# Queries and keys of the attention loaded through SyncE's hardware queue as plain 32-bit numbers

## The chip, the core and the metric

The kernel runs on one core of a Trainium2 chip. A core has TensorE (PE, matrix products), VectorE (DVE), ScalarE (ACT), GpSimd (POOL) and SyncE (SP), and 16 DMA engines that move data between its on-chip memory (SBUF, 128 partitions) and DRAM. SP issues transfers through the hardware queue, GpSimd through the software queue. The metric is the time of one execution on the chip, in microseconds (us); lower is better.

## What is computed

One layer of a decoder trunk over 1040 tokens (16 learned ones and 1024 of the sequence), width 1024. Four mixers work on columns of one projection: windowed attention (A), differential attention (B), a recurrent mixer (C, RWKV-7) and a convolution module (D). Then come an output projection, a router and 16 experts.

```python
u = h @ w_in
ya = swa_attention(qa, ka, va, sinks, rel_a)     # 4 query heads on 2 key heads, 64 wide, window 128
yb = diff_attention(qd, kd, vd, lam, ...)        # 4 heads, two softmax maps each, 32 wide
yc = rwkv7_mix(uc, ...)                          # state carried from chunk to chunk
yd = conv_module(ud, ...)
h = LN(alpha * h + concat(ya, yb, yc, yd) @ w_out)
h = LN(alpha * h + moe(h))
```

The change concerns the inputs of A and B: their queries and keys.

## The kernel before

The kernel has three stages. The first (to about 257 us) normalises the input and computes the recurrent mixer's and the convolution's projections. The second holds the attention's projections, the recurrence in 17 chunks of 64 tokens, the attention over 8 blocks of 128 queries, and the output projection with the router. The third, from about 1000 us, runs the experts. Their weights stream through SP's queue.

In the second stage a planner (`Steps.run`) sets the order of the work. Each piece of work is a step with an engine, a guessed cost, what it depends on, and the buffers that it takes (`RINGS`, `SZ`). The planner always takes the step that can start first by its own guesses, and writes its instructions at that place. So the order on every engine is fixed when the program is built. An engine works strictly in that order and stands still where an instruction's data isn't there, whatever could run behind it.

The path of queries and keys. `project` and `qk_evac` compute them in parts: ScalarE writes the rounded part `qhi` (type float32r), VectorE the remainder `qlo`, and SP stores both to the DRAM array `dqk` [7, 2, 128, 1040] (L869, L870), as float32. Each row is 1040 numbers, 4160 bytes. After the last projection `load_qk` (L1280) reads them back, one step for each of six head groups `s`: 0 and 1 are the windowed attention's two key heads, 2 to 5 the four differential heads. Each group fills four buffers `qk0` to `qk3` of 128 partitions and 1040 numbers. Groups 0 and 1 do it in four transfers of 128 rows, groups 2 to 5 in eight of 64 rows. The source is read with an outermost count of 2, for instance the two remainders behind each other (`[WS, 2]`) or the same rows twice (`[0, 2]`). The buffers have the type float32r and the source float32; a transfer that changes the type goes through GpSimd's software queue. `SZ["qk0"]` to `SZ["qk3"]` are 2, so two groups are on the chip at a time.

The order of use (`ORDER`): groups 0 and 2 together, block by block; then groups 1 and 3; then 4 and 5. The scores are computed at L1340 and L1341 (windowed) and at L1444 and L1424 (differential). Between them stand pieces of the recurrence: `prep` (L928 to L1013) and `chain` (L1045 to L1105), whose inputs SP loads at L903 and L904. `values` (L1254) loads the attention's values.

DMAs of one queue share eight semaphores in turn, so the ninth transfer is issued once the first has landed.

Of the kernel before, what the change touches and what calls it, by code (L numbers as in the profile page):

```python
# [9 lines left out]
F32 = mybir.dt.float32  # L10
# [15 lines left out]
NT = S + M  # L26
# [166 lines left out]
def build(tc, A, out, dbg=None, upto=99):  # L193
# [3 lines left out]
    V, G, ACT, T, SY = nc.vector, nc.gpsimd, nc.scalar, nc.tensor, nc.sync  # L197
# [492 lines left out]
    a = add("DVE", .1, lambda: V.memset(relx, NEG), (), TB)  # L690
# [14 lines left out]
    a = add("DVE", .7, tb_neg, [tl_], TB)  # L705
# [26 lines left out]
    a = add("Pool", 1.6, empty, [tl_], TB, use=[scy])  # L732
# [60 lines left out]
    st_ = Steps(RINGS)  # L793
# [16 lines left out]
    def at_(name, shape, dt=F32):  # L810
        return ap_.tile([P] + shape, dt, name=name, bufs=RINGS.get(name) or SZ[name])
# [300 lines left out]
    class Norms:  # L1112
# [5 lines left out]
        def add(self, y, deps):  # L1118
            add, pr = st_.add, self.pr
            w, s1_, s2_, w.s3 = O(), Slot("tp"), Slot("tp"), Slot("sq")  # L1120
            w.y = y

            def a1():
                w.a = bank2("tp")
                T.matmul(w.a, bdm, y, start=True, stop=True)

            def a2():
                V.tensor_tensor(y, y, w.a, op=ALU.subtract)

            def a3():  # L1130
                w.sq = rt("sq", [512])
                ACT.activation(w.sq, y, AF.Square)

            def a4():
                w.a = bank2("tp")
                T.matmul(w.a, bdm, w.sq, start=True, stop=True)

            def a5():
                ACT.activation(w.sq, w.a, AF.Ln, bias=self.eps)
            a = add("PE", .9, a1, deps, pr, take=[s1_])  # L1140
            a = add("DVE", dve(512), a2, [a], pr, use=[s1_])
            a = add("ACT", act(512), a3, [a], pr, take=[w.s3])
            a = add("PE", .9, a4, [a], pr, take=[s2_], use=[w.s3])
            self.logs.append(add("ACT", act(512), a5, [a], pr, use=[s2_, w.s3]))
            self.w.append(w)
            return w
# [131 lines left out]
    qkb, qkl, qks = {}, {}, {}  # L1278

    def load_qk(s, deps):  # L1280
        WS = P * NT

        def ld(dst, i, w, r, n, outer):
            a = dqk[i, w, r:r + n]
            G.dma_start(dst, bass.AP(tensor=a.tensor, offset=a.offset, ap=outer + [[NT, n], [1, NT]]))  # L1285

        def go():
            t = qkb[s] = [at_(f"qk{z}", [NT], F32R) for z in range(4)]
            if s < 2:
                r = 64 * s  # L1290
                for w in range(2):
                    ld(t[w], 2, w, r, 64, [[0, 2]])
                    ld(t[2 + w], w, 0, r, 64, [[WS, 2]])
            else:
                hp_, hh_ = divmod(s - 2, 2)
                for c in range(2):
                    r = 64 * hh_ + 32 * c
                    for z in range(2):
                        ld(t[c][64 * z:64 * z + 64], 3 + hp_, 0, r, 32, [[WS, 2]])
                        ld(t[2 + c][64 * z:64 * z + 64], 5 + hp_, z, r, 32, [[0, 2]])  # L1300
        qks[s] = Slot("qk")
        qkl[s] = st_.add("Pool", 4 if s < 2 else 8, go, deps, 1, take=[qks[s]])
    for z in range(4):
        SZ[f"qk{z}"] = 2

# [283 lines left out]
    for ct in range(2):  # L1589
# [3 lines left out]
        for q, w in enumerate(cw_):  # L1593
            conv_silu(ct, q, w, last)
    sw = [st_.add("SY", 0, switch, sp_, 0)]
    load_qk(0, sw)
    tabs = [st_.add("SY", 6, tables, after, 30)]
    tabs = [st_.add("DVE", 1.6, far_bias, tabs, 5)]
    vals = sum([values(i, 0.6 + .1 * i, sw) for i in range(3)], [])
    for s in (2, 1, 3, 4, 5):  # L1600
        load_qk(s, sw)
# [44 lines left out]
    def high(i):  # L1646
        ACT.activation(slot_h[i % HLS][0], raw[i], AF.Copy)  # L1647

    def low(i, eng):
        h, l = slot_h[i % HLS]  # L1650
        eng.tensor_tensor(l, raw[i], h.bitcast(F32), op=ALU.subtract)  # L1651
        free_r.append(raw.pop(i))
# [363 lines left out]
    for i, eng in enumerate(PREL):  # L2016
        a = add("ACT", act(D), lambda i=i: high(i), (wdone if i >= NEW else []) + [raws[i]] + (sgd[-1:] if i >= HEARLY else []), SB + 20 + i)
        a = add(eng, dve(D) if eng == "DVE" else pol(D), lambda i=i, eng=eng: low(i, V if eng == "DVE" else G), [a] + ((ixd if i >= DEARLY else lnd)[-1:] if eng == "DVE" else []), SB + 20 + i)
# [187 lines left out]
    st_ = Steps(dict(st=2))  # L2206
# [45 lines left out]
    for half in range(2):  # L2252
# [3 lines left out]
        a = add("ACT", .35, lambda h=h, half=half: ACT.activation(B.act[:, h], B.a[half][:, 0:256], AF.Silu), [last], -20)  # L2256
        sl_.append(a)
        a = add("DVE", .35, lambda h=h, half=half: V.tensor_tensor(B.act[:, h], B.act[:, h], B.a[half][:, 256:512], op=ALU.mult), [a], -20)
# [6 lines left out]
        a = add("PE", .22, t1, [a], -20)  # L2265
        a = add("ACT", .3, lambda v=v, h=h: ACT.activation(B.at[:, 0, h], v.tb[:, :256], AF.Copy), [a], -20)
# [17 lines left out]
    a = add("DVE", .2, lambda: V.bn_aggr(mv[:, NB], B.st), [zs[-1]], -5, use=[zst])  # L2284
    c = add("ACT", .3, lambda: root(NB, NB + 1), [a] + sl_, -5)
    a = add("DVE", dve(D), lambda: V.scalar_tensor_tensor(B.y, B.y, mv[:, NB, 0:1], g2r, op0=ALU.subtract, op1=ALU.mult), [a], -5)
# [94 lines left out]
```

## Time and profile before

| | |
|---|---|
| median of 3 runs | 1639.62 us (1634.83 to 1651.75) |
| the profiled execution's own time | 1646.74 us |
| its span, first to last instruction | 1645.0 us |
| TensorE busy (8079 matmuls) | 1321.9 us, 80% |
| VectorE, ScalarE, GpSimd busy | 945.1, 636.3, 519.2 us |
| mean granted clock of TensorE | 0.858 of full speed |
| DMA, hardware queue | 176.25 MB, 34.2% of 16 engines |
| DMA, software queue | 41.73 MB, 14.1% of 16 engines |
| issues at L1285 on POOL | 40, 27.7 us busy, 715 ns each |

The profile is one execution. "Busy" is the time in which an engine works; issuing a DMA counts on POOL here and doesn't on SP. Other views break it down by time: the waits (who waited for whom), the timeline of an engine, and windows, which give for each stretch the busy time of every engine, the granted TensorE clock (1.00 is 2.4 GHz, 0.50 is 1.2 GHz), the mean share in which the 16 DMA engines were busy, and the GB/s that they moved.

### The profile page before, as it was taken

How to read it: one execution, taken by the hardware profiler on the slowest of the kernel's cores; microseconds unless marked ns; L12 is line 12 of the kernel's file. 1: busy time of each engine (PE TensorE's matmuls, PEld its weight loads, DVE VectorE, ACT ScalarE, POOL GpSimd, SP SyncE). 2: the span in 40 equal slices, each digit the busy share in tenths (PEclk: the TensorE clock that was granted, in tenths of full speed). 3: DMA queues.
4: the chain of work that ended last, by engine and by line, in shares of the span. 5: the costliest groups of instructions: out<-in, count | busy, mean ns of one | idle time of the engine just before them, and what ended most of it. 6: DMA issues, size and time to landing. Idle time of an engine off the chain costs nothing. (4 is left out here: it accounts for less than half of the span.)

```text
span 1645.0 us, 22192 instructions
## 1 busy us (share of the span) xinstructions
PE 1321.9 (80%) x8079; PEld 1071.5 (65%) x8079; DVE 945.1 (57%) x1628; ACT 636.3 (39%) x1108; POOL 519.2 (32%) x382
## 2 busy tenths in 40 slices
PE   6908999999859949968967885779799789978980
PEld 4807899887738738756836764557577567756860
DVE  8307658883214433646856768574744774465466
ACT  6204412323113333425663313444544554454351
POOL 3303214322110121233325233442544354344323
PEclk9958999999955767977969977779899899989995
DMA  7431246221480070090023336586877797586652
GB/s 179 88 50 65 82 119 195 82 79 54 94 123 1 17 100 23 1 105 20 2 103 117 126 77 220 158 267 197 281 230 218 227 316 229 151 262 208 203 168 115
DMA packets 186403, 220.14 MB, mean 134 GB/s; under 512 B 56903, under 2 KB 155335, under 8 KB 185976
## 3 DMA queue, kind: packets, MB, share of 16 engines
q1 hardware_dynamic: 152328, 176.25, 34.2%
q0 software_dynamic: 33904, 41.73, 14.1%
q8 instruction: 93, 1.52, 0.4%
q14 instruction: 78, 0.64, 0.1%
HBM read 172.41 MB, written 45.44 MB: 132 GB/s over the span
## 5 line engine op out<-in xcount | busy, mean ns | idle before, releaser
L452 PE MATMUL acc<-hh,wh 128*128 128x256 f32 (+2 forms) x288 | 97.8, 340 | 0.0
L452 PE MATMUL acc<-hh,wl 128*128 128x256 f32 (+2 forms) x288 | 93.7, 326 | 0.0
L1651 DVE TENSOR_TENSOR wl<-MX,wh 128x1024 fp32r<-128x1024 f32 x46 | 85.4, 1892 | 13.6 <-ACT wh L1647 13.1
L452 PE MATMUL acc<-hl,wh 128*128 128x256 f32 (+2 forms) x288 | 87.7, 323 | 0.0
L2095 PE MATMUL rw<-wh,at 128*128 128x512 f32 x224 | 81.0, 411 | 6.2 <-DVE at L2071 5.8
L1169 DVE SCALAR_TENSOR_TENSOR CY<-MX,cvw,CY 128x1024 f32<-128x1024 f32 x60 | 82.5, 1399 | 0.2
L1647 ACT ACTIVATE wh<-MX 128x1024 fp32r<-128x1024 f32 x66 | 66.3, 1048 | 10.9 <-PEq L2142 10.9
L1651 DVE TENSOR_TENSOR wol<-MX,woh 128x1024 fp32r<-128x1024 f32 x33 | 60.3, 1863 | 12.6 <-ACT woh L1647 11.0
L1462 ACT ACTIVATE E<-sc,nm 128x144 f32<-128x144 f32 (+7 forms) x64 | 48.0, 750 | 50.3 <-DVE nm L1456 45.4
L1486 POOL TENSOR_TENSOR E<-E,rho 128x272 f32<-128x272 f32 (+3 forms) x16 | 20.5, 1281 | 147.9 <-DVE rho L1480 107.1
L2099 POOL DMA_INDIRECT acc__131<-y,ixs x21 | 34.4, 1637 | 103.4 <-issue 64.7
L835 POOL TENSOR_TENSOR wl<-raw,wh 128x1024 fp32r<-128x1024 f32 x10 | 26.3, 2628 | 115.2 <-ACT wh L832 106.4
L2071 DVE TENSOR_TENSOR at<-tp,at 128x256 fp32r<-128x256 f32 x46 | 19.4, 422 | 73.7 <-ACT at L2070 73.7
L452 PEld LDWEIGHTS acc<-hh,wh 128*128 128x128 f32 x288 | 55.8, 194 | 5.8 <-issue 5.5
L1800 PE MATMUL oacc<-wol,mh 128*128 128x512 f32 x128 | 54.2, 423 | 5.8 <-POOL wol L1747 4.0
L1800 PE MATMUL oacc<-woh,mh 128*128 128x512 f32 x128 | 56.2, 439 | 1.7 <-ACT woh L1744 1.7
L1285 POOL DMA_DIRECT2D qk<-dqk x40 | 27.7, 715 | 93.6 <-DMA qk<-dqk 53.1
L452 PEld LDWEIGHTS acc<-hh,wl 128*128 128x128 f32 x288 | 55.6, 193 | 1.7 <-issue 1.0
L1647 ACT ACTIVATE woh<-MX 128x1024 fp32r<-128x1024 f32 x51 | 51.7, 1049 | 12.3 <-PEq L2142 8.5
L2095 PEld LDWEIGHTS rw<-wh,at 128*128 128x128 f32 x224 | 42.2, 191 | 18.3 <-DVE at L2071 8.4
L452 PEld LDWEIGHTS acc<-hl,wh 128*128 128x128 f32 x288 | 53.8, 190 | 0.0
L1800 PE MATMUL oacc<-woh,ml 128*128 128x512 f32 x128 | 53.4, 417 | 0.0
(474 smaller groups left out, 3923.7 us busy)
## 6 DMA issues: line engine op xcount, KB each, us to landing
MX<-in_exp_w_dram SPq DMA_DIRECT2D x192, 256.0 KB
MX<-in_exp_w_dram SPq DMA_DIRECT2D x48, 512.0 KB
CY<-in_exp_w_dram SPq DMA_DIRECT2D x64, 256.0 KB
raw<-in_w_in_dram SPq DMA_DIRECT2D x20, 512.0 KB
qk<-dqk POOLq DMA_DIRECT2D x32, 260.0 KB, 15.4
CY<-in_exp_w_dram SPq DMA_DIRECT2D x16, 512.0 KB
dab<-ab SPq DMA_DIRECT2D x2, 2176.0 KB
qk<-dqk POOLq DMA_DIRECT2D x8, 520.0 KB, 27.5
```

What stands on the lines that cost most here:

```text
L452: T.matmul(v.acc[:, :wid], wt[:, k], x[:, k, c0:c0 + wid], start=(z + y == 0 and wt is w.h), stop=(z + y == len(ks) - 1))
L835: G.tensor_tensor(w.l, w.raw, w.h.bitcast(F32), op=ALU.subtract)
L1169: V.scalar_tensor_tensor(y, hc[:, M + j:M + j + S], cvw[:, ct, j:j + 1], y, op0=ALU.mult, op1=ALU.add)
L1285: G.dma_start(dst, bass.AP(tensor=a.tensor, offset=a.offset, ap=outer + [[NT, n], [1, NT]]))
L1462: ACT.activation(w.E[:, c, off:W], w.sc[c][:, :W - off], AF.Exp, bias=w.nm[:, c:c + 1], scale=-1.0, accum_out=w.s[:, c:c + 1])
L1486: G.tensor_tensor(w.E[:, 1, :W], w.E[:, 1, :W], w.rho.to_broadcast([P, W]), op=ALU.mult)
L1647: ACT.activation(slot_h[i % HLS][0], raw[i], AF.Copy)
L1651: eng.tensor_tensor(l, raw[i], h.bitcast(F32), op=ALU.subtract)
L1800: T.matmul(v.o, x_[:, k], y_[k][:, 512 * n:512 * n + 512], start=(i == 0 and j == 0), stop=(i == KT - 1 and j == 2))
L2071: V.tensor_tensor(dst[:, 1, s], tb[:, :m * P], dst[:, 0, s].bitcast(F32), op=ALU.subtract)
L2095: T.matmul(o[n], at[:, x, k * P:(k + 1) * P], w[k][y][:, n * 512:n * 512 + 512], start=(k == 0 and (x, y) == (0, 0)), stop=(k == 3 and x = ...
L2099: G.indirect_dma_start(out=acc_, out_offset=bass.IndirectOffsetOnAxis(ap=ix[:, 0:1], axis=0), in_=y, in_offset=None, compute_op=ALU.add)
```

## The change

The 40 loads of `load_qk` are issued by SP instead of GpSimd. The destination is passed as float32 (`bitcast`), so that no type is changed in the transfer. The planner sees the step on SP, with other guessed costs.

```diff
         def ld(dst, i, w, r, n, outer):
             a = dqk[i, w, r:r + n]
-            G.dma_start(dst, bass.AP(tensor=a.tensor, offset=a.offset, ap=outer + [[NT, n], [1, NT]]))
+            SY.dma_start(dst.bitcast(F32), bass.AP(tensor=a.tensor, offset=a.offset, ap=outer + [[NT, n], [1, NT]]))
...
-        qkl[s] = st_.add("Pool", 4 if s < 2 else 8, go, deps, 1, take=[qks[s]])
+        qkl[s] = st_.add("SY", 3 if s < 2 else 5, go, deps, 1, take=[qks[s]])
```

On SP, the loads of groups 0 and 2 now stand behind the three loads of the values (the number behind `qk_` is the buffer's; 128x1x1040 is the shape written):

```order
 L1254 DMA E<-dvv 128x1040 x3
+L1285 DMA qk_3715<-dqk 128x1x1040
+L1285 DMA qk_3717<-dqk 128x1x1040
+L1285 DMA qk_3716<-dqk 128x1x1040
+L1285 DMA qk_3718<-dqk 128x1x1040
+L1285 DMA qk_3761<-dqk 64x1x1040
+L1285 DMA qk_3763<-dqk 64x1x1040
```

Six more of group 2 follow, and behind them the recurrence's next loads (L903, L904), which stood right behind L1254 before. On POOL the same loads are gone from between the recurrence's products (L1053):

```order
 L1053 TENSOR_SCALAR sp_3356<-s_3316,pend 128x64 x2
-L1285 DMA qk_3592<-dqk 128x1x1040
-L1285 DMA qk_3594<-dqk 128x1x1040
-L1285 DMA qk_3593<-dqk 128x1x1040
-L1285 DMA qk_3595<-dqk 128x1x1040
-L1053 TENSOR_SCALAR sp_3647<-s_3618,pend 128x64 x2
-L1285 DMA qk_3661<-dqk 64x1x1040
```

Since the guessed costs differ, the planner also shifts other work by a few places on every engine. On PE, where the second pair of groups is used first (group 1 at L1340, group 3 at L1444), before:

```order
L928 MATMUL prep<-abv 128x128 x4
L1506 MATMUL tp<-c__63,E 128x128 x7
L1506 MATMUL tp<-c__63,E 16x128
L982 MATMUL prep<-Tt,gs 64x64 x8
L1367 MATMUL tp<-c__63,Es 128x128 x4
L982 MATMUL prep<-X,um 64x64 x8
L1526 MATMUL tp<-vs,at 128x128 x7
L1527 MATMUL tp<-vs,at 128x128
L1068 MATMUL chain<-r,X 64x64 x4
L1375 MATMUL tp<-c__63,Es 16x128 x2
L1444 MATMUL sc<-qk_4662,qk_4660 128x144
```

These rows stand right behind the first L1340 and L1341 of group 1. In the changed kernel the same place reads:

```order
L1341 MATMUL sc<-qk_4533,qk_4535 128x144
L982 MATMUL prep<-Tt,gs 64x64 x8
L1506 MATMUL tp<-c__63,E 128x128 x7
L1506 MATMUL tp<-c__63,E 16x128
L982 MATMUL prep<-X,um 64x64 x8
L1444 MATMUL sc<-qk_4672,qk_4670 128x144
L1444 MATMUL sc<-qk_4673,qk_4671 128x144
```

L928 has moved ahead of L1340, and both first L1444 of group 3 have moved up, ahead of L1367, L1526 and the recurrence's chain.

## Rows read from the trace of the kernel before

**Rows 1.** Waits of PE, 440 to 800 us: engine, line, waited for; us, times, longest.
```profile
PE sc L1340 <- DMA qk<-dqk: 38.9, 2, 19.8
...
PE tp L1424 <- DMA qk<-dqk: 12.1, 3, 7.1
...
PE sc L1444 <- DMA qk<-dqk: 3.1, 1, 3.1
```

**Rows 2.** Timeline of PE: start, us, line, output<-input, count, [idle before <- what ended it].
```profile
469.40 0.46 PE L1340 MATMUL sc<-qk,qk 128*128 128x144 f32 x1 [19.84 <-DMA qk<-dqk]
...
486.73 0.46 PE L1444 MATMUL sc<-qk,qk 128*128 128x144 f32 x1 [3.06 <-DMA qk<-dqk]
...
487.12 2.07 PE L928 MATMUL prep<-abv 64*128 64x128 f32 x8
...
608.61 0.46 PE L1340 MATMUL sc<-qk,qk 128*128 128x144 f32 x1 [19.07 <-DMA qk<-dqk]
...
616.04 1.12 PE L982 MATMUL prep<-X,um 64*64 64x64 f32 x16
...
723.18 0.35 PE L1424 MATMUL tp<-qk,qk 128*128 128x16 f32 x1 [1.79 <-DMA qk<-dqk]
...
735.70 0.35 PE L1424 MATMUL tp<-qk,qk 128*128 128x16 f32 x1 [7.12 <-DMA qk<-dqk]
...
739.21 0.35 PE L1424 MATMUL tp<-qk,qk 128*128 128x16 f32 x1 [3.15 <-DMA qk<-dqk]
```

**Rows 3.** Timeline of POOL, the issues of the queries' and keys' loads.
```profile
440.07 3.46 POOL L1285 DMA_DIRECT2D qk<-dqk  x4 [23.12 <-PE acc L849]
...
447.13 2.68 POOL L1285 DMA_DIRECT2D qk<-dqk  x4
...
580.77 3.24 POOL L1285 DMA_DIRECT2D qk<-dqk  x4 [12.99 <-PE sc L1341]
...
586.56 2.60 POOL L1285 DMA_DIRECT2D qk<-dqk  x4 [2.54 <-PE sc L1444]
...
698.91 5.30 POOL L1285 DMA_DIRECT2D qk<-dqk  x8 [1.71 <-PE sc L1341]
```

**Rows 4.** The page's part on DMA issues: queue, count, KB each, us to landing.
```profile
qk<-dqk POOLq DMA_DIRECT2D x32, 260.0 KB, 15.4
...
qk<-dqk POOLq DMA_DIRECT2D x8, 520.0 KB, 27.5
```

**Rows 5.** Windows, four then eight loads in flight; at the end clock, DMA share, GB/s.
```profile
583.00:585.00 2.00, 2.00 (x14) 1.64 (x14) 1.54 (x7) 1.49 (x7) 1.01 (x2) 1.00 0.61 53
...
600.00:603.00 3.00, 0.00 (x0) 0.00 (x0) 0.00 (x0) 0.00 (x0) 0.00 (x0) 0.50 1.31 124
```

**Rows 6.** Timeline of SP, two stores at L719; below it windows while they drain.
```profile
54.34 10.52 SPq L719 DMA_DIRECT2D skew<-MX  x2
...
68.00:72.00 4.00, 4.00 (x28) 4.00 (x27) 0.48 (x1) 1.82 (x3) 0.00 (x0) 1.00 0.45 52
...
88.00:92.00 4.00, 0.00 (x0) 0.00 (x0) 0.00 (x0) 0.00 (x0) 0.00 (x0) 0.52 0.23 26
```

**Rows 7.** Windows, loads of x and w_in alone at the start.
```profile
5.00:6.00 1.00, 0.00 (x0) 0.00 (x0) 0.84 (x2) 0.00 (x0) 0.00 (x0) 1.00 1.00 377
...
6.00:8.00 2.00, 0.00 (x0) 0.00 (x0) 1.65 (x4) 0.29 (x1) 0.00 (x0) 1.00 1.01 401
```

**Rows 8.** Timelines of SP and PE: loads of the values, and their first use.
```profile
440.67 1.76 SPq L1254 DMA_DIRECT2D E<-dvv  x3
...
447.07 1.87 PE L1267 MATMUL tp<-c__63,E 128*16 128x128 f32 x8
```

**Rows 9.** The page's part on DMA queues: packets, MB, share of 16 engines.
```profile
q1 hardware_dynamic: 152328, 176.25, 34.2%
```

**Rows 10.** Windows, the clock after the first stall: busy us (count), clock, DMA, GB/s.
```profile
480.00:530.00 50.00, 46.94 (x272) 38.16 (x272) 19.71 (x80) 15.87 (x54) 1.40 (x2) 0.50 0.13 27
...
545.00:550.00 5.00, 5.00 (x57) 4.16 (x58) 2.83 (x10) 3.15 (x10) 0.76 (x2) 0.95 0.00 2
```

## The prediction

> **What bounds the kernel now.** I read the waits of TensorE first, over 440 to 800 us, the stretch in which the queries and keys are loaded [rows 1]. In every row the left part waits and the arrow names what ended the wait. Only three rows have a DMA of `qk` behind them: 38.9 us at L1340 (scores of the windowed attention), 12.1 us at L1424 and 3.1 us at L1444 (scores of the differential attention). These 54 us are all that a faster load could give back directly, 3.3% of the span.
>
> The timeline of PE places them [rows 2]; the bracket is idle time ahead of the instruction. There are three stalls, one for each pair of loads: 19.84 and 3.06 us before 469.40 and 486.73, about 19 us before 608.61, and 1.79, 7.12 and 3.15 us before 723.18, 735.70 and 739.21. The timeline of POOL gives the issue times [rows 3]: head groups 0 and 2 from 440.07, groups 1 and 3 from 580.77 and 586.56, groups 4 and 5 from 698.91. The bracket there says that each pair starts when PE has read a buffer for the last time, so a load can't start earlier just because another queue issues it: there are two buffers.
>
> How are the transfers slow? The page's part on issues gives landing times of 15.4 us for 260 KB and 27.5 us for 520 KB [rows 4], 17 to 19 GB/s for one transfer. Next come stretches with four and with eight of them in flight [rows 5]. With four the DMA engines are 0.61 busy, with eight 1.31 (packets overlap, so a share passes 1). Twice the transfers, twice the engines: one transfer keeps about two of the sixteen, and the software queue gives each the next two. Eight in flight move 124 GB/s in that window, though each alone crawls.
>
> **The change part by part.**
>
> *Removed from POOL:* 40 issues of about 0.7 us, 28 us in all. None of PE's three waits names POOL's work behind an issue; where POOL stands held by its next issue, PE waits for the same transfers. Worth 0, and the cover is PE's own wait; without it, the 28 us.
>
> *The change of type:* gone; the hardware queue copies the bits. What that is worth depends on the engines that a transfer gets, next.
>
> *Added to SP's queue:* 40 issues, in order, behind the three loads of values. They delay the recurrence's loads behind them (L903, L904), but the group loaded next is first read by PE after the second pair of loads, so this costs 0 unless the queue is late by another 80 us. The xg and bo loads are read later still.
>
> *How a transfer is spread.* The source pattern of `ld` has an outermost count of 2 in every call ([0, 2] or [WS, 2]). The trace has two stores on the same SP queue with small outermost counts, L719: 8 rows and then 4, each repeated 128 times, issued one after the other [rows 6]. While the first drains, the DMA share stays at 0.45, close to 8 engines of 16; from 88 us it is 0.23, close to 4 of 16. The second didn't run beside the first on other engines, or the share would have been about 0.7 while both were open, and nothing would have been left of it at 88 us. So on this queue the outermost count sets the number of engines, and successive transfers get the same ones. For `qk` that means two engines, and the same two for all twelve transfers of a pair, which then run one after another.
>
> The Trainium skill (DMA: Bandwidth & Descriptors, section "Why a DMA increments its semaphore by 16 and not by 1") states this as a rule: the number of engines is the largest up to 16 that divides both patterns' slowest dimension, on the hardware queue the lowest-numbered ones, on the software queue consecutive ones from a moving cursor. [rows 5, 6] agree with both halves. By it the sum is the one worked out here from rows.
>
> *Rate of two engines.* No row shows a two-engine load. Nearest: x and w_in loads on SP with all engines full, 377 to 401 GB/s at a share of 1.00 [rows 7], 25 GB/s for an engine. Lower bounds: the hardware queue's average over the span, 176.25 MB in 34.2% of 16 engines over 1645 us, 19.6 GB/s [rows 9]; and the loads of values, whose rows have the same 4160 bytes, three of 520 KB from 440.67 and read at 447.07 [rows 8], 250 GB/s or 15.6 for an engine, with the qk traffic beside them. The upper end is little over 25, say 27, since full engines never show more. I take 25: plain large rows with nothing else running is the case here. One head group is 8 x 260 KB or 4 x 520 KB, 2.13 MB, so 2.13 / 0.050 = 42.6 us; a pair takes 85 us, where it took some 40 to 46.
>
> *Pair 1.* The values are in by about 447 [rows 8], so group 0 lands at 490 and group 2 at 532. In the new order PE has done by its second L1444 what it did up to 487.12 before, and besides the L928 of that row (2.07), four L982 pieces (1.12 each, as in the row at 616.04) and a product with the values (some 3 us), together 10 us: before, that point would be at 497. Cost 532 - 497 = 35.
>
> *Pair 2.* From 580.8: group 1 at 623, group 3 at 666. In the new order both first L1444 of group 3 come right behind the first L1340 block and two L982. Before, PE had got that far at about 616 [rows 2]. Cost 666 - 616 = 50. The first half, 623 against 608.61, is in it.
>
> *Pair 3.* From 698.9: group 4 at 741.5, group 5 at 784. Before, the last wait for group 5 ended at 739.21; the new order does some 3 us more work ahead of it. Cost 784 - 742 = 42.
>
> Sum: 35 + 50 + 42 = 127 us. The profiled execution took 1646.7 us (span 1645.0), which makes 1774; that run is 7 us above the median, 1639.6, on which the sum gives 1767. Some microseconds of landing time for the last transfer of each pair are in none of these terms; I say 1770. With 27 GB/s a group takes 39.4 us and each pair 6 less: 108. With 19.6 it takes 54.3, each pair 23 more: 197. With 15.6, 68, 51 more: 280.
>
> *TensorE's clock.* It falls to 0.50, the lower of its two levels, in the first stall, and stays there for 480 to 530 although PE is busy 46.9 of 50 us; at 545 it is at 0.95 again [rows 10]. Longer stalls could stretch or shift such stretches: a stretch like that one done at the full level would save some 23 us, one more of them cost as much. I put 0 in the sum and 30 us either way in the range.
>
> **The rivals.**
>
> *1, faster: the loads spread over all engines.* If the hardware queue splits loads by the destination's 128 or 64 partitions (the stores of [rows 6] had their small count on the SBUF side, these have it on the DRAM side), 2.13 MB at 400 GB/s takes 5.3 us and a pair 11. All three stalls go: 1640 - 54 = 1586, with the clock's 23 about 1563. For it: loads on SP do reach 400 GB/s [rows 7]. Against: the software queue's shares [rows 5] follow the count of 2 on these very patterns. It decides from where a pair lands as quickly as today, 43 us or 100 GB/s, four full engines; above that the kernel gets faster.
>
> The Trainium skill's same page ("Issuing engine by pattern") puts simple loads on SyncE and calls that path generally faster; by this rule the result would be this rival's.
>
> *2, no change: about four engines' worth.* Two engines for each transfer, but the pairs partly shared out, so that a pair takes about 43 us. Then the stalls stay as they are, 1640. Only a middle course between [rows 5] and [rows 6] gives it.
>
> *3, much slower: two engines at the software queue's pace.* If 9 GB/s an engine [rows 4] comes from the 4160-byte rows and not from the change of type, a pair takes some 235 us and the sum is near 580: 2220. Against it: the loads of values, 15.6 an engine at least [rows 8].
>
> **How the numbers follow.** Forecast (two engines, 15 to 27 GB/s each) 0.81; rival 1 0.10; rival 2 0.05; rival 3 0.04. The low end is 108 less 30 for the clock, on 1640: 1718, so 1715. The high end is the 19.6 GB/s case with the clock, 1640 + 197 + 30 = 1867, and part of what lies toward 15.6: 1880. It holds the forecast but for its slow tail, about 0.78. A change of 1% is about what can be told from none here: faster 0.10, within 1% 0.05, slower 0.85.
>
> **What would show it.** In the new profile the DMA share beside `qk` alone stays near 0.13, two of sixteen, at some 50 GB/s; PE waits for `qk` in three places with 150 to 190 us in all; the second group of each pair lands about 85 us after the first is issued; nothing changes before 440 and after the attention. A share above 0.5 there, or waits under 54 us, proves the step on the spread wrong; the right share with another rate shows the rate mis-sized; long waits on abv or vch show that I was wrong on SP's queue.

## The result and the profile after

The changed kernel takes 1752.47 us (median of 4 runs, 1737.36 to 1762.66); the kernel before takes 1637.22 us beside it (4 runs, 1634.32 to 1651.75). The ratio is 1.068, 95% interval 1.057 to 1.079: slower by 115 us. The forecast was 1770, between 1715 and 1880. In a later run on one chip with others (after_same, below) the ratio was 1.072 [1.066, 1.077]. The profiled execution took 1745.57 us, its span is 1743.8 us, 98.8 us more than the span of before.

I read the same views in the same order. First the waits of PE over 440 to 920 us, the stretch that answers to [rows 1]. Columns: engine, line, what was waited for; us, times, longest.

```profile
PE sc L1444 <- DMA qk<-dqk: 67.7, 4, 21.7
PE sc L1340 <- DMA qk<-dqk: 40.6, 4, 12.8
PE tp L1424 <- DMA qk<-dqk: 33.5, 2, 19.7
PE sc L1341 <- DMA qk<-dqk: 19.3, 2, 9.7
...
PE tp L1424 <- issue: 6.3, 1, 6.3
```

161 us behind a DMA of `qk`, where it was 54. No row names `abv` or `vch`, the recurrence's loads that now stand behind the twelve on SP's queue. The timeline of PE shows the pace (the bracket is idle time ahead of the instruction), where [rows 2] had one to three stalls for each pair:

```profile
470.21 0.49 PE L1340 MATMUL sc<-qk,qk 128*128 128x144 f32 x1 [12.76 <-DMA qk<-dqk]
480.39 0.49 PE L1341 MATMUL sc<-qk,qk 128*128 128x144 f32 x1 [9.70 <-DMA qk<-dqk]
490.59 0.49 PE L1340 MATMUL sc<-qk,qk 128*128 128x144 f32 x1 [9.70 <-DMA qk<-dqk]
...
511.31 0.46 PE L1444 MATMUL sc<-qk,qk 128*128 128x144 f32 x1 [10.34 <-DMA qk<-dqk]
533.47 0.46 PE L1444 MATMUL sc<-qk,qk 128*128 128x144 f32 x1 [21.70 <-DMA qk<-dqk]
...
676.22 0.46 PE L1444 MATMUL sc<-qk,qk 128*128 128x144 f32 x1 [19.65 <-DMA qk<-dqk]
...
830.33 0.35 PE L1424 MATMUL tp<-qk,qk 128*128 128x16 f32 x1 [19.71 <-DMA qk<-dqk]
```

470.21, 480.39, 490.59: one load of 520 KB lands every 10.2 us, 52 GB/s, while others stand behind it. The timeline of SP gives the issues (start, us, line, count), which answers to [rows 3]:

```profile
443.57 69.56 SPq L1285 DMA_DIRECT2D qk<-dqk  x12
513.23 4.77 SPq L903 DMA_DIRECT2D abv<-dab  x1
...
591.45 66.49 SPq L1285 DMA_DIRECT2D qk<-dqk  x12
...
744.99 66.48 SPq L1285 DMA_DIRECT2D qk<-dqk  x16
```

Twelve issues take 66 to 70 us: the ninth waits for the first to land, and so on. The last load of the second pair lands 676.22 - 591.45 = 84.8 us after the pair's first issue, that of the third pair 830.33 - 744.99 = 85.3 us after; the forecast was 85. Windows show the engines (the last three numbers are granted clock, DMA share, GB/s). First two stretches in which `qk` is alone, then from the last load of pair 1 to the issue of pair 2, and from the last load of pair 2 to the issue of pair 3:

```profile
465.00:470.00 5.00, 0.00 (x0) 0.00 (x0) 0.00 (x0) 0.00 (x0) 0.00 (x0) 0.50 0.13 52
615.00:635.00 20.00, 0.95 (x2) 0.57 (x2) 0.00 (x0) 0.00 (x0) 0.00 (x0) 0.50 0.13 52
...
533.47:591.45 57.98, 55.87 (x500) 44.32 (x501) 38.95 (x136) 31.77 (x88) 11.21 (x13) 0.93 0.05 15
676.22:744.99 68.77, 67.96 (x630) 55.64 (x630) 38.34 (x141) 30.24 (x91) 9.52 (x11) 0.93 0.04 11
```

Share 0.13 is two of sixteen engines, 26 GB/s each; with four transfers in flight on the software queue it was 0.61 [rows 5]. The other two rows are compared below with the same stretches of before, counted from the points that the prediction had taken for equal (497 and 616):

```profile
496.70:580.77 84.07, 83.50 (x603) 65.25 (x604) 37.72 (x129) 29.34 (x80) 11.45 (x13) 0.65 0.03 9
616.00:698.91 82.91, 82.21 (x745) 66.36 (x744) 43.05 (x153) 33.24 (x100) 16.91 (x21) 0.87 0.05 13
```

In the page's part on queues the hardware queue has taken over the loads' bytes, 12.8 MB more than in [rows 9], at no larger a share of the span:

```profile
q1 hardware_dynamic: 155480, 189.03, 33.9%
```

Where the 98.8 us between the two profiled runs lie, by the issues and the last product of L1444: up to the issue of pair 2 591.45 - 580.77 = 10.7; from there to the issue of pair 3 (744.99 - 591.45) - (698.91 - 580.77) = 35.4; from there to the last L1444 (918.82 - 744.99) - (831.78 - 698.91) = 41.0; the rest of the span (1743.8 - 918.82) - (1645.0 - 831.78) = 11.8.

Two kernels below have no ratio (pool_plain, pool_rows_plain): three of the four runs of each fell in a slower state of the chip, so what is read of them is how long the loads took to land.

### The profile page after: what moved, and what is told of

It is laid out like the page before. It is cut to its first block, busy times and chain, and to the rows that moved or that the text cites. A ratio compares the mean times of both kernels' runs of the same rounds, so it can differ in the third digit from the quotient of the medians.

```text
span 1743.8 us, 22157 instructions
## 1 busy us (share of the span) xinstructions
PE 1294.4 (74%) x8079; PEld 1049.8 (60%) x8079; DVE 930.8 (53%) x1628; ACT 635.1 (36%) x1108; POOL 491.4 (28%) x342
## 3 DMA queue, kind: packets, MB, share of 16 engines
q1 hardware_dynamic: 155480, 189.03, 33.9%
q0 software_dynamic: 8688, 28.87, 7.1%
## 5 line engine op out<-in xcount | busy, mean ns | idle before, releaser
L1444 PE MATMUL sc<-qk,qk 128*128 128x512 f32 (+3 forms) x104 | 35.6, 415 | 69.4 <-DMA qk<-dqk 67.7
L1651 DVE TENSOR_TENSOR wl<-MX,wh 128x1024 fp32r<-128x1024 f32 x46 | 78.3, 1737 | 13.4 <-ACT wh L1647 12.1
L1444 PEld LDWEIGHTS sc<-qk,qk 128*128 128x128 f32 x104 | 18.1, 204 | 75.3 <-issue 69.6
```

What stands on the lines that cost most here:

```text
L1444: T.matmul(w.sc[c][:, f0:f1_], Q[:, t0:t0 + P], K[:, off + f0:off + f1_], start=True, stop=True)
```

## The experiments

Theory A is the prediction's: the outermost count of the source pattern sets how many DMA engines a load gets, on SP's queue always the same ones. The rivals were B, that SP's queue gives such a load 52 GB/s however it is described; C, that the planner's new order costs the time; and that the change of type had made the old loads slow.

**The order alone** (order_only). The changed kernel, but the load's line is that of before; the planner still treats the step as SP's.

```diff
-            SY.dma_start(dst.bitcast(F32), bass.AP(tensor=a.tensor, offset=a.offset, ap=outer + [[NT, n], [1, NT]]))
+            G.dma_start(dst, bass.AP(tensor=a.tensor, offset=a.offset, ap=outer + [[NT, n], [1, NT]]))
```

> The changed kernel's order on every engine (planned on SP with its guessed costs), but the loads go through GpSimd's software queue with the change of type again. Theory A (the outermost count of 2 keeps each load on two DMA engines, on SP's queue always the same two): the order costs nothing, waits for qk near the 54 us of before, time 1637 within 20. Rival C (the planner's new order is what costs): near 1752.

Measured: 1632.55 us, ratio 0.994 [0.987, 1.000]. The order costs nothing that can be told. C falls; the loss is in the loads. The waits for `qk` were not near 54 us, as I had expected, but 33.5 (over 440 to 800 us, in the shortest of ten runs): if anything the new order helps.

**The change of type alone** (pool_plain). The kernel before, with the destination passed as plain numbers.

```diff
-            G.dma_start(dst, bass.AP(tensor=a.tensor, offset=a.offset, ap=outer + [[NT, n], [1, NT]]))
+            G.dma_start(dst.bitcast(F32), bass.AP(tensor=a.tensor, offset=a.offset, ap=outer + [[NT, n], [1, NT]]))
```

> The kernel before, with one edit: the destination is passed as float32, so the software queue copies without a change of type. Order as before. Theory A: still two engines a load, but moving on from load to load; without the change of type each moves 52 GB/s as on SP instead of 19, so a 520 KB load lands in some 10 to 12 us instead of 27.5, a pair in under 20 us, the waits for qk fall from 54 to about 20: 1600 to 1615. If the slowness of before came from the 4160-byte rows or the queue and not from the type: 1637, landing times unchanged.

Measured: no ratio; one run took 1623.83 us, beside 1626.11 to 1646.31 of before. The page's part on DMA issues (queue, count, KB each, us to landing) is that of [rows 4]:

```profile
qk<-dqk POOLq DMA_DIRECT2D x32, 260.0 KB, 15.6
...
qk<-dqk POOLq DMA_DIRECT2D x8, 520.0 KB, 28.0
```

15.6 and 28.0 us, with the change of type 15.4 and 27.5. My expectation of a gain from faster landings was wrong: the 9 GB/s for each engine that looked like the price of the conversion doesn't come from it.

**The description alone** (sp_rows, sp_four, sp_eight). The changed kernel, the same bytes into the same buffers; within a buffer the rows fall on other partitions, in the same order for queries and keys. In sp_rows the rows are the slowest dimension; in sp_four and sp_eight each load is issued as two, each with its rows cut in 4 or in 8.

```diff
-            SY.dma_start(dst.bitcast(F32), bass.AP(tensor=a.tensor, offset=a.offset, ap=outer + [[NT, n], [1, NT]]))
+            SY.dma_start(dst.bitcast(F32), bass.AP(tensor=a.tensor, offset=a.offset, ap=[[NT, n]] + outer + [[1, NT]]))
```

and in sp_four (sp_eight has 8 in place of 4):

```diff
-            SY.dma_start(dst.bitcast(F32), bass.AP(tensor=a.tensor, offset=a.offset, ap=outer + [[NT, n], [1, NT]]))
+            for z in range(2):
+                SY.dma_start(dst[n * z:n * z + n].bitcast(F32), bass.AP(tensor=a.tensor, offset=a.offset + z * outer[0][0], ap=[[NT, 4], [4 * NT, n // 4], [1, NT]]))
```

> The changed kernel, same 40 loads on SP in the same order, but the source pattern has the 64 or 32 rows outermost and the count of 2 inside; rows land in another order of partitions, the same one for queries and keys. Theory A: all 16 engines, share near 1.0 and 400 GB/s, a group lands in 5 to 7 us, waits for qk under 15 us in all: 1560 to 1600, faster than both kernels. Rival B (SP's queue gives such a load 52 GB/s however it is described, for instance one transfer at a time): 1752 as the changed kernel, share 0.13. Rival C (the order costs): also 1752.

> As the changed kernel, but each load is two, one for each half of its partitions, with an outermost count of 4 (every fourth row); 80 loads of the same bytes. Theory A: four engines, share 0.26, about 104 GB/s, a group in 21 us and a pair in 41, as long as before: 1637 within 25. Rival B: 52 GB/s again, 1752 or, if the rate hangs on the number of loads, more. If the halving itself freed all engines: share near 1 and 1560 to 1600.

> The changed kernel with each load issued as two, one for each of the two blocks, and each with its slowest dimension cut in eight, [NT, 8], [8 NT, n/8]: eight engines by theory A, where sp_four had four. Expected by A: a DMA share of 0.5 and some 205 GB/s while the loads run alone (0.13 and 52 in the changed kernel, 0.26 and 105 in sp_four), a pair in some 21 us or what the 24 issues take, whichever is longer; waits of TensorE for qk under 15 us and a time of 1590 to 1615, near the 1592 of sp_rows. By B (the queue's own pace) share and time would stay those of sp_four, 1640.

Measured: sp_four 1639.77 us, ratio 0.999 [0.993, 1.004]; sp_eight 1606.22, ratio 0.973 [0.967, 0.978]; sp_rows 1591.78, ratio 0.974 [0.962, 0.986]. Windows while their loads run, first of sp_four, then of sp_eight, then four of sp_rows (three in its first pair, the last in its third):

```profile
590.00:600.00 10.00, 1.72 (x18) 1.22 (x17) 1.89 (x6) 1.01 (x4) 5.27 (x5) 0.50 0.26 104
```

```profile
550.00:555.00 5.00, 3.63 (x33) 2.78 (x29) 3.54 (x11) 1.87 (x7) 4.00 (x2) 0.65 0.51 206
```

```profile
447.00:453.00 6.00, 6.00 (x41) 4.27 (x39) 0.29 (x1) 2.06 (x6) 0.00 (x0) 0.50 1.04 346
...
447.00:449.00 2.00, 2.00 (x17) 1.53 (x15) 0.29 (x1) 1.31 (x4) 0.00 (x0) 0.50 1.02 418
...
453.00:459.00 6.00, 6.00 (x51) 4.70 (x52) 0.70 (x3) 3.12 (x10) 0.86 (x2) 0.62 1.04 223
...
629.00:637.00 8.00, 6.89 (x74) 5.56 (x74) 5.47 (x16) 4.24 (x13) 0.86 (x2) 0.88 1.04 216
```

Outermost count 2, 4, 8, then 64 or 32: share 0.13, 0.26, 0.51, 1.04 and 52, 104, 206, then 346 or 216 GB/s. A is shown, B falls: it is the same queue with the same bytes. The time follows as the prediction's rivals had it: at four engines' worth nothing changes, above it the kernel gets faster. In sp_rows the waits of PE for `qk` are down to one row:

```profile
PE sc L1444 <- DMA qk<-dqk: 3.0, 1, 3.0
```

**The software queue with rows outermost** (pool_rows; pool_rows_plain without the change of type). The kernel before, on its own queue and in its own order.

```diff
-            G.dma_start(dst, bass.AP(tensor=a.tensor, offset=a.offset, ap=outer + [[NT, n], [1, NT]]))
+            G.dma_start(dst, bass.AP(tensor=a.tensor, offset=a.offset, ap=[[NT, n]] + outer + [[1, NT]]))
```

> The kernel before (software queue, change of type, the order of before) with one edit: in ld the rows are the slowest dimension of the source's pattern, [NT, n] + outer + [1, NT], as in sp_rows. Theory A, the description sets how many DMA engines a load gets on either queue: a load spreads over all sixteen, the first group lands within some 12 us of its first issue instead of 30, TensorE's 54 us of waits for qk fall under 15, and the time is 1590 to 1615. Theory B, the software queue has a pace of its own per load (17 to 19 GB/s whatever the description): the landing times stay at 15 and 27 us, the waits at 54 us, the time at 1640 to 1650. Theory D, the change of type costs once the engines are no longer the limit: between, 1615 to 1640, and then pool_rows_plain is faster.

> As pool_rows, but without the change of type: the tile is written as plain 32-bit numbers. It tells what the change of type costs when the description is no longer in the way. Theory A: nothing, within 8 us of pool_rows (1590 to 1615). Theory D: the change of type takes time in the DMA engines, so this one is 10 to 40 us faster than pool_rows. Theory B: as the kernel before, 1640 to 1650.

Measured: pool_rows 1590.91 us, ratio 0.964 [0.957, 0.971]. The page's issues:

```profile
qk<-dqk POOLq DMA_DIRECT2D x32, 260.0 KB, 7.8
...
qk<-dqk POOLq DMA_DIRECT2D x8, 520.0 KB, 7.2
```

520 KB land in 7.2 us instead of 27.5. The software queue had no pace of its own, and with the change of type it does as well as SP's queue without. pool_rows_plain has landing times of 8.1 and 8.6 us and took 1587.99 in its profiled run: no gain from dropping the change of type that could be told. The page's part on queues (packets, MB, share) shows what else the description does on the software queue, first pool_plain, then pool_rows, then the changed kernel, in which these loads aren't on it:

```profile
q0 software_dynamic: 33904, 41.73, 13.0%
```

```profile
q0 software_dynamic: 12400, 41.65, 12.0%
```

```profile
q0 software_dynamic: 8688, 28.87, 7.1%
```

The loads are 33904 - 8688 = 25216 packets with the count of 2 outermost and 12400 - 8688 = 3712 with the rows. The 21504 that fall away hold 0.08 MB, some 4 bytes each. SP's queue has 155480 - 152328 = 3152 packets for the same loads with the count of 2 outermost. Whether the small packets set the software queue's pace wasn't tried.

**The queue alone** (sp_rows_old). The order of before, rows outermost, on SP's queue: pool_rows with the other queue.

```diff
-            G.dma_start(dst, bass.AP(tensor=a.tensor, offset=a.offset, ap=outer + [[NT, n], [1, NT]]))
+            SY.dma_start(dst.bitcast(F32), bass.AP(tensor=a.tensor, offset=a.offset, ap=[[NT, n]] + outer + [[1, NT]]))
```

> The kernel before with the line of ld changed to SyncE's queue, plain numbers and rows as the slowest dimension, in the order of before. With pool_rows (software queue, same description, same order, 1591) it tells what the queue itself is worth, and so whether the 28 us of issues taken from GpSimd were worth 0 as predicted. If they are: 1585 to 1605, within 10 us of pool_rows. If they cost something hidden behind the slow loads so far: 1565 to 1580. If SyncE's queue pays for them, since the values' loads now stand between the twelve: 1605 to 1620.

Measured: 1591.63 us, ratio 0.967 [0.961, 0.974], beside 0.964 [0.957, 0.971] of pool_rows. So the queue itself, and the 28 us of issues taken from GpSimd, are worth nothing that can be told.

**The order under slow loads, and the clock** (sp_old_order, sp_old_same, after_same). The first two are one kernel, run twice: before with only the load's line changed, so that every engine keeps its old order. after_same is the changed kernel itself.

```diff
-            G.dma_start(dst, bass.AP(tensor=a.tensor, offset=a.offset, ap=outer + [[NT, n], [1, NT]]))
+            SY.dma_start(dst.bitcast(F32), bass.AP(tensor=a.tensor, offset=a.offset, ap=outer + [[NT, n], [1, NT]]))
```

> The kernel before with only the line of ld changed: SyncE's queue, plain numbers, the description with a slowest count of 2; the planner still plans the step as it did for the software queue, so every engine keeps the order of the kernel before. If the new order has no part in the loss: 1740 to 1765, like the changed kernel, with the same 85 us for a pair. If the new order saved what the prediction gave too much (pair 1 was forecast at 35 us and cost 11; the same work after the first stall ran at the higher clock): the first pair costs some 25 us more than in the changed kernel, 1770 to 1790. If the order itself cost time: under 1735.

> The changed kernel itself, beside sp_old_same on one chip, since what the order gave is a difference of two ratios whose intervals overlap (1.068 and 1.079). Theory C1, the new order gives back some 25 us in the first pair because TensorE is back at its full clock 25 to 30 us sooner after the stall: 1740 to 1760 here, 20 to 35 us under sp_old_same, and in the trace the first pair of loads ends near 533 while the second pair is issued near 591. Theory C2, the difference of the two earlier runs is scatter between chips and hours: within 8 us of sp_old_same.

> sp_old_order again (the kernel before with only the line of ld changed), beside after_same. C1: 1770 to 1790, 20 to 35 us over after_same; the first pair of loads ends near 535, the clock stays at 0.50 until about 570, the second pair is issued near 619. C2: within 8 us of after_same.

Measured: sp_old_order 1779.25 us, ratio 1.079 [1.073, 1.085]. Side by side: after_same 1761.78, 1.072 [1.066, 1.077]; sp_old_same 1769.79, 1.080 [1.075, 1.085]. The new order saves some 8 us here; the intervals overlap, so its size stays open, between nothing and some 20 us. The 25 us that C1 wanted is not shown. Windows from the last load of pair 1 to the issue of pair 2 tell why; the first fence is before, then sp_old_order, sp_old_same, after_same (the changed kernel's own row stands above, 58 us at a clock of 0.93):

```profile
486.73:580.77 94.04, 93.47 (x638) 73.43 (x640) 42.26 (x147) 31.19 (x88) 11.45 (x13) 0.63 0.03 10
```

```profile
535.90:619.05 83.15, 82.58 (x633) 64.79 (x631) 42.83 (x149) 31.82 (x91) 11.46 (x13) 0.73 0.03 9
```

```profile
536.88:605.64 68.76, 67.93 (x634) 52.79 (x631) 42.92 (x149) 31.98 (x92) 11.45 (x13) 0.93 0.04 11
```

```profile
531.71:599.45 67.74, 65.62 (x500) 52.22 (x501) 39.35 (x136) 31.90 (x88) 11.21 (x13) 0.77 0.04 13
```

The first three rows are the same work (633 to 638 products) in 94, 83 and 69 us, at mean clocks of 0.63, 0.73 and 0.93. The changed kernel does its 500 products in 58.0 us at 0.93 in one execution and in 67.7 at 0.77 in another. TensorE falls to the lower of its two levels in the stall, in all of them; when it comes back differs from one execution of the same program to the next, near 542 in one execution of the changed kernel and near 563 in the other (windows of 5 us). C1 falls: I had read one execution's clock as an effect of the order.

## Why the prediction was right

**What bounds the kernel.** Right, but for a fourth row of 0.2 us at L1341 that was left out. With the 54 us of waits gone (sp_rows) the attention ends 831.78 - 758.46 = 73 us sooner: the waits, and a clock of 0.84 instead of 0.70 over 440 to 700 us, with hardly a stall left. Of the 73 some 58 reach the end of the span (1645.0 - 1586.5).

**How a transfer is spread.** Right, and shown by the series 2, 4, 8, rows. The prediction took it from two stores whose tails kept shares of 0.45 and 0.23 [rows 6]. The Trainium skill (DMA: Bandwidth & Descriptors, section "Why a DMA increments its semaphore by 16 and not by 1") has the engines follow the slowest dimension; shares of 0.13, 0.26, 0.51 and 1.04 agree with it.

**Rate of two engines.** Taken as 25 GB/s each; measured 26. Pairs 2 and 3 took 85 us, as forecast, and pair 1 was in within 1.5 us of the forecast; the two bounds below 25 weren't needed.

**The change of type and POOL's issues at 0.** Both right (pool_plain; sp_rows_old beside pool_rows). SP's queue at 0: right, nobody waited for `abv` or `vch`.

**Pair 1: 35 forecast, 10.7 measured.** The loads were right: the last landed at 533.5, forecast 532. What lies behind them was mis-sized twice. The point taken as equal, 497, had 603 products left up to the issue of pair 2 before and 500 after (windows above), and the clock over them was 0.65 before and 0.93 after. sp_old_same tells the two apart: it has the order of before, so the point that answers to 497 can be found in it (542.54), and it does the same work near the upper level:

```profile
542.54:605.64 63.10, 62.27 (x595) 48.09 (x594) 38.50 (x131) 29.64 (x83) 11.45 (x13) 0.92 0.05 12
```

So the clock is worth 84.07 - 63.1 = 21.0 us, and the new order the 63.1 - 58.0 = 5.1 that are left. 35 + 1.5 - 21.0 - 5.1 is 10.4. The order's part lies on both sides: from the start of the span before had done 2869 products at 497 and 3470 at the issue of pair 2, the changed kernel 2912 at its last landing and 3412 at that issue. So 43 products more stood ahead of the stall than I counted, and 58 more are left until pair 2 is under way. The prediction put the clock at 0, 30 us either way: as a term of the range that was right, and the price of a stretch at the lower level too (23 us; 94.0 against 68.8 here, 25 us).

**Pair 2: 50 forecast, 35.4 measured.** The same step: 745 products left before, 630 after, at a clock of 0.87 and 0.93, in 82.9 and 68.8 us, 14.1 less. At the price of pair 1 (21.0 us for 0.27 of the clock) the 0.06 are some 5 us, an estimate, and the order some 9; no run tells them apart. The landing was 84.8 instead of 85.2 us after the issue. 50 - 0.4 - 14.1 = 35.5.

**Pair 3: 42 forecast, 41.0 measured.** The loads were right; that the term fits to 1 us is luck. In after_same the four stretches cost 18.7, 38.3, 49.7 and 13.1 us where they cost 10.7, 35.4, 41.0 and 11.8 here, with the same program.

**After the attention: 0 forecast, 11.8 measured.** Not explained. This stretch took 813 us in before, 825 in after, 826 in after_same, 828 in sp_rows and 844 in pool_rows, so it moves by more than that with fast loads too. The clock over all of it is 0.87 in before and after, 0.86 in sp_rows and 0.85 in pool_rows; in its first 200 us it is 0.82 in before and 0.79 in after, and the experts' first product at L2068 comes 5 us later behind the last L1444.

**The sum.** 127 us forecast, 98.8 between the two profiled executions, 115 and 121.5 (1761.78 - 1640.28) between medians. The forecast was near because the terms of the loads were right, and in part by luck: the first two pairs were 40 us too dear (26.1 and 14.1, the clock and the order), and the unexplained 12 made up for some of it. The profiled execution of before lay above its median, that of after below.

**The rivals.** 1 (all sixteen engines) is not what the change does, but sp_rows makes it so: 1592 where 1586 was worked out without the clock and 1563 with it. There, and in pool_rows, either queue serves. The Trainium skill (DMA: Bandwidth & Descriptors, section "Issuing engine by pattern") puts simple loads on SyncE and calls that path generally faster; these runs don't bear it out, with 0.967 on SyncE's queue (sp_rows_old) and 0.964 on GpSimd's (pool_rows). 2 (four engines' worth, no change) is sp_four: 104 GB/s and 0.999, at the point of 100 GB/s that the prediction named. 3 (9 GB/s an engine) is shown wrong by 26.

## What to carry to other kernels

Before a load is moved between queues or its conversion is dropped, read its source pattern: with a small outermost count it crawls on a few DMA engines, and on SP's queue the next load crawls behind it on the same ones. The cure here was one line, the rows as the slowest dimension, and it helped either queue (to 0.974 of the kernel before from 1.068 on SP's, to 0.964 on GpSimd's). When a stall is predicted from a trace, count the instructions between it and the next issue in the old order and in the new one, price them by time and not by number, and keep the clock as a range of its own: one execution can't tell an effect of the order from the clock's.

## What the runs showed of the hardware

- On the software queue the pace of 9 GB/s for each engine [rows 4, 5] isn't the change of type: without it the landing times were the same, and with rows outermost 520 KB land in 7.2 us with it. With the count of 2 outermost this queue carries seven more packets, of some 4 bytes, for each row of 4160 bytes (21504 for the 3072 rows of the 40 loads); SP's queue doesn't.
- With all sixteen engines busy the rate still differs: in the first pair of sp_rows it is 418 GB/s at first, where by the order of the issues loads of 520 KB (128 partitions) are under way, and 223 behind 453 us, where loads of 260 KB follow, which fill 64 partitions each. In the third pair, all of 260 KB, it is 216. The share is 1.02 to 1.04 in all three. Whether the partitions are the reason wasn't tried.
- After a stall the clock's return to its upper level differs by some 20 us between two executions of one program, with the same products in the same order (58.0 and 67.7 us); half a per cent of the span between two profiles can be this alone.
